# One step of a hybrid decoder layer on one core: cached keys handed over features leading, gathers spread over one-head-wide rows, gate groups moved between stages

## The chip, the cores and the metric

The kernel runs on one core of a Trainium2 chip. The time is device microseconds (us) of one execution, given as the median of several. A profile is one further execution, recorded by the hardware profiler; its span runs from its first to its last instruction. TensorE (PE) does matrix products, its weight loads (PEld) overlap them; VectorE (DVE), ScalarE (ACT) and GpSimd (POOL) do the element-wise work, SyncE (SP) issues most transfers. [...]

## The reference

288 tokens (a prompt of 256, and 8 sequences of 4 new tokens) go through one layer of width 4096. Cut to what matters:

```python
m = jax.nn.silu(c) @ w_ada + b_ada                  # (9, 4096) @ (4096, 12288): "adaLN"
shift, scale, gate = jnp.split(m[:, None, :], 3, axis=-1)
h = _rmsnorm(x, g_norm) * (1 + scale) + shift
(u_a, v_a, z_a, qkv_b, z_b, a_b, b_b, q_c, k_c, v_c, z_c, qi_c, ki_c, wi_c) = _split_in(h @ w_in)
...                                                  # mixer A: gMLP over chunks of 128, times silu(z_a)
qkv_conv, conv_new = _causal_conv(qkv_b, conv_prev, dn_conv_w)
o_b, s_new = _gated_delta(...)                       # mixer B: 16 heads, delta rule, times silu(z_b)
o_c = attend(q_c, k_c, v_c, qi_c, ki_c, wi_c)        # mixer C, times silu(z_c)
mix = jnp.concatenate([y_a, y_b, y_c], axis=-1)
x = x + gate * (mix @ w_out)                         # then a last RMSNorm

def _sparse_attend(q, k_sel, v_sel, valid):          # of mixer C, new tokens against their cache:
    s = jnp.einsum('bthgd,btkhd->bthgk', q, k_sel).astype(jnp.float32) * C_HEAD ** -0.5
    s = jnp.where(valid[:, :, None, None, :], s, -jnp.inf)
    p = jax.nn.softmax(s, axis=-1)
    return jnp.einsum('bthgk,btkhd->bthgd', p.astype(v_sel.dtype), v_sel)
```

The cache is paged: 8 sequences of 16 pages, a page being 128 positions of 2 key heads of 128 features (float32); a page table says which page of a pool of 160 is which. An indexer picks the keys that each query may see; the kernel scores all 2048 cached positions and masks the others.

## The kernel before

**Products.** All tokens stand as 288 columns. A weight tile of 128 x 1024 is loaded from HBM (`w`, four buffers, 512 KB a load), cast to a shorter float by ACT (`wh`), the rest is found by DVE (`wl`), and TensorE multiplies three times into one bank of PSUM (`acc`): hH by wh, hL by wh, hH by wl. A "block" is 128 output columns. Four of PSUM's banks (acc 0 to 3) are for these sums, four others for all else, which the code calls "banks". "A group" is four blocks (512 columns); the group called c, 112 columns of small things, is one block wide.

**Stages, in TensorE's order.** Stage 1 ("p1") computes m, with c as the stationary operand (`ada<-wa`, weight tiles `wa`, five buffers), interleaved with the first groups of the input projection. m arrives in order of the features, so the input projection is done here in 11 steps over the features (six of 2 tiles of 128, then five of 4); in each step every group of this stage adds its partial sum to SBUF (`part_finish`, DVE: `zb<-zb,acc`, `v_c` and the like). The groups are c, qi0, qi1, kv, qc0, qc1 and the gate groups that `PLAN["p1"]` names (zc: gates of mixer C, zb of B, za of A, each name 512 columns). Stage 2 takes the gate groups of `PLAN["attn"]`, then q, k and v of mixer B in four groups of heads (12 groups of columns, `qkv_finish`, `conv_gen`, each group's chain `dn_all`, DN[0] to DN[3]), then `PLAN["dn3"]`, then mixer A's v and u. The last stage multiplies the mix by w_out, eight groups, features in the order KB = 2, 3, 4, 5, 6, 7, 0, 1 (blocks of 512; each is loaded as `mx` from `mixD` and split into mH and mL by `mix_gen`). The gate third of m (`ada<-w`) is spread over stage 2.

**Who decides the order.** The products of the weights follow a written list of units. Everything else (attention, delta rule, indexing, gathers) runs as generators which a planner, `Weaver`, advances between these units by a clock of its own, with a guessed time for each instruction and transfer (`note_dma`: a gather counts as landed 4 us after its issue). `W.finish([...])` at a unit emits the rest of a chain there, with no weight product in between: `end_prev` does it for DN[g-2] at the end of group g's q columns, `gmlp_open` for DN[3], at unit 12 of mixer A's last u group. All engines execute in their own program order.

**The cached keys** (`sample_gen`, two halves of four sequences). Per half, 16 gathers on POOL's queue fetch 128 rows of 4 KB each (`kraw`; four positions of both heads in a row, row numbers `ixk` made by `idx_prompt`'s part for the cache). Each is transposed by 8 products with the identity (`kT`), copied from PSUM by DVE and ACT (`ktk`) and multiplied with the queries (`S<-ktk,qS`, 16 matmuls of 32 rows), then copied into S by ACT twice. The values come in 32 gathers per half of 128 rows of 2 KB (`vraw`), used as they are. POOL also does 1/9 of each convolution (`tap`, `cv`, 32 columns).

Of the kernel before, what the change touches and what calls it, by code (L numbers as in the profile page):

```python
# [12 lines left out]
I32 = mybir.dt.int32  # L13
AF = mybir.ActivationFunctionType
OP = mybir.AluOpType
# [24 lines left out]
N_RAW, N_ADA, N_SPLIT = 4, 5, 4  # L40
# [6 lines left out]
LEAD0 = 0  # L47
GMO = 12
# [5 lines left out]
PLAN = {"p1": ["zc0", "zc1", "zb0", "zb1", "zb2", "zb3"], "attn": ["za0", "za1"], "dn3": []}  # L54
# [36 lines left out]
class Weaver:  # L91
# [98 lines left out]
    def note_dma(self, key, out, ins):  # L190
        t = self.t
        t[key] = max([t[key], self.at(out, but="D"), self.at(out, None, self.reads), self.born.get(out.tensor.name, 0.0)] +
                     [self.at(x) for x in ins]) + (1.0 if key == "G" else 0.05)
        q = t[key]
        if key != "G":
            n = self.n_dma % 8
            q = t[key] = max(q, self.lanes[n])
            q = t["H"] = max(t["H"], q) + 0.45
        d = out.shape[0] * _size(out) * 4 / 360e3
        if key == "G":  # L200
            e, t["D"] = max(t["D"], q + 0.6) + d, t["D"] + d
        else:
            e = t["D"] = max(t["D"], q + 0.6) + d
            self.lanes[n] = e + 1.2
            self.n_dma += 1

        self.used(self.parts, out, e + (4.0 if key == "G" else 2.0), "D")
        for x in ins:
            self.used(self.reads, x, e + 1.2, "D")
# [172 lines left out]
def tile_hybrid_step(ctx: ExitStack, tc: tile.TileContext, I, O):  # L382
# [79 lines left out]
    class Gemm(Unit):  # L462
# [21 lines left out]
        def mm(self, j):  # L484
            us = [self.with_, self] if self.with_ else [self]
            if j == 0 and us[0].first:
                self.st.acc = {}
            off, m = self.tiles[j]
            if us[0].first:
                self.st.acc[j] = acc_tile(j)  # L490
            acc = self.st.acc[j]
            for u in us:
                kk = u.kk
                xh, xl = self.XH[kk // 4][:, kk % 4], self.XL[kk // 4][:, kk % 4]
                a, b = u.wh[:, off:off + m], u.wl[:, off:off + m]
                T.matmul(acc[:m, :NTOK], a, xh, start=u.first, stop=False)
                T.matmul(acc[:m, :NTOK], a, xl, start=False, stop=False)
                T.matmul(acc[:m, :NTOK], b, xh, start=False, stop=u.last)
            if self.last:
                self.finish(j, acc)  # L500
# [369 lines left out]
    while i < len(lb):  # L870
        rate, nxt = max([((min(len(la), la_end[j] + LEAD) - n) / (at_[j] - at_[i]), j) for j in range(i + 1, len(lb))],
# [269 lines left out]
    def idx_sample_gen():  # L1141
# [7 lines left out]
        sub16 = tl("ap", [P, 1], "sub16")  # L1149
        V.memset(sub16, 0.0)  # L1150
        sv = tl("ap", [P, 4], "sv")
        V.memset(sv, 16.0)

        for q in range(4):
            G.affine_select(sv[:, q:q + 1], sv[:, q:q + 1], pattern=[[0, 1]], compare_op=OP.is_ge, fill=0.0,
                            base=-32 * q - 16, channel_multiplier=1)
            G.affine_select(sv[:, q:q + 1], sv[:, q:q + 1], pattern=[[0, 1]], compare_op=OP.is_ge, fill=0.0,
                            base=32 * q + 31, channel_multiplier=-1)
# [9 lines left out]
        ptm = pts[:, 384:448].rearrange("p (b j) -> p b j", j=16)  # L1168
        G.memset(ptm, 0.0)
        for u in range(2):  # L1170
            G.affine_select(ptm, ptm, pattern=[[-32, 4], [-1, 16]], compare_op=OP.not_equal, fill=1.0,
                            base=-16 * u, channel_multiplier=1)
# [5 lines left out]
        V.tensor_reduce(sub16, sv, axis=AX.X, op=OP.max)  # L1178
        ptf = tl("ap", [P, 3], "ptf")
# [4 lines left out]
        V.tensor_tensor(ptT.rearrange("p (h n) -> p h n", h=2), ptF.rearrange("p (h n) -> p h n", h=2),  # L1184
                        pts[:, 384:448][:, None].to_broadcast([P, 2, 64]), op=OP.mult)
        V.tensor_reduce(ptf[:, 1:3], ptT.rearrange("p (h n) -> p h n", h=2), axis=AX.X, op=OP.add)
# [5 lines left out]
        X.ixk = tl("ap", [P, 2, 16], "ixk", 1, I32)  # L1192
        for hf in range(2):
            V.tensor_scalar(ptf[:, 1 + hf:2 + hf], ptf[:, 1 + hf:2 + hf], 32.0, sub16, op0=OP.mult, op1=OP.add)
            V.tensor_scalar(X.ixk[:, hf], iof, ptf[:, 1 + hf:2 + hf], None, op0=OP.add)
# [208 lines left out]
    def sample_gen():  # L1404
        yield lambda: hasattr(X, "qready")
        k_rows = I["cache_k"][0].rearrange("n (e l) h d -> (n e) (l h d)", e=32)
# [3 lines left out]
        def gather_k(hf, s):  # L1410
            raw = tl("ap", [P, 4, 256], "kraw", 2)
            G.indirect_dma_start(out=raw.rearrange("p l c -> p (l c)"), out_offset=None, in_=k_rows,
                                 in_offset=bass.IndirectOffsetOnAxis(ap=X.ixk[:, hf, s:s + 1], axis=0))
            return raw
# [16 lines left out]
        for hf in range(2):  # L1431
# [3 lines left out]
            raws = [gather_k(hf, 0), gather_k(hf, 1)]  # L1435

            def qk_lane(par):
                raw = raws[par]
                for s in range(par, 16, 2):
                    yield [raw]  # L1440
                    yield from bank(2)
                    pk = [pr4("kT") for _ in range(2)]
                    for kv in range(2):
                        for l in range(4):
                            T.transpose(pk[kv][:, l], raw[:, l, kv * HD:(kv + 1) * HD], ident)
                    if s + 2 < 16:
                        raw = gather_k(hf, s + 2)
                    yield [pk[1]]
                    kt = tl("ap", [P, 2, 4, P], "ktk", 2, tag="kt")
                    V.tensor_copy(kt[:, 0], pk[0])  # L1450
                    A.copy(kt[:, 1], pk[1])
                    free(2)
                    yield from bank()
                    ps = pr("S")
                    qk_mm(ps, P, hf, lambda kv, bb: kt[:, kv, :, 32 * bb:32 * bb + 32])
                    yield
                    dst = Sk[:, 4 * (s % 4):4 * (s % 4) + 4].rearrange("p l (j u w) -> p l w u j", u=2, w=4)[:, :, s // 4]
                    for u in range(2):
                        A.activation(dst[:, :, u], ps[:, 0:P].rearrange("p (l u j) -> p u l j", l=4, u=2)[:, u], AF.Copy,
                                     scale=HD ** -0.5)  # L1460
                    free()

            ls = W.push(qk_lane(0), qk_lane(1), front=True)
            yield lambda: all(x.done for x in ls)
# [915 lines left out]
_INS = ["x_prompt", "x_sample", "cache_k", "cache_v", "cache_kidx", "state_dn_t", "state_conv_t", "page_table",  # L2380
# [9 lines left out]
def lay_out(inputs):  # L2390
# [3 lines left out]
    a = dict(inputs)  # L2394
    a["state_conv_t"] = np.asarray(a.pop("state_conv"))[0].reshape(24, 12, 4, P).transpose(1, 3, 2, 0)
# [52 lines left out]
```

## Time and profile before

| what | value |
|---|---|
| time, median of 3 runs | 2605.29 us (2603.06 to 2607.48) |
| the profiled execution's own time | 2601.98 us |
| its span | 2600.3 us |
| TensorE busy | 2498.2 us (96%) |
| VectorE, ScalarE, GpSimd busy | 1622.6, 1055.8, 478.0 us |
| granted TensorE clock, mean | 0.983 |
| moved over DMA | 615.88 MB, mean 237 GB/s |

A busy time is the sum of an engine's instructions in the span; matrix products overlap each other, so the mean of one (296 ns) is longer than the step from one to the next.

### The profile page before, as it was taken

How to read it: one execution, taken by the hardware profiler on the slowest of the kernel's cores; microseconds unless marked ns; L12 is line 12 of the kernel's file. 1: busy time of each engine (PE TensorE's matmuls, PEld its weight loads, DVE VectorE, ACT ScalarE, POOL GpSimd, SP SyncE). 2: the span in 40 equal slices, each digit the busy share in tenths (PEclk: the TensorE clock that was granted, in tenths of full speed). 3: DMA queues.
4: the chain of work that ended last, by engine and by line, in shares of the span. 5: the costliest groups of instructions: out<-in, count | busy, mean ns of one | idle time of the engine just before them, and what ended most of it. 6: DMA issues, size and time to landing. Idle time of an engine off the chain costs nothing. (4 is left out here: it accounts for less than half of the span.)

```text
span 2600.3 us, 51897 instructions
## 1 busy us (share of the span) xinstructions
PE 2498.2 (96%) x19572; PEld 2232.4 (86%) x19572; DVE 1622.6 (62%) x3616; ACT 1055.8 (41%) x2446; POOL 478.0 (18%) x1096
## 2 busy tenths in 40 slices
PE   5999999999999999999999999999999998999997
PEld 3788888888897788888899889989989988999997
DVE  3377765555568798555576576667567566555554
ACT  3423223323344434344444444444454534444443
POOL 1000000000001122534533333443330200000000
PEclk9999999999999999999999999999999999999998
DMA  7988988887656567877776565666666455555554
GB/s 281 369 328 340 343 321 316 314 326 298 220 182 207 169 224 255 284 255 259 252 261 204 171 224 204 203 218 222 200 219 236 143 198 163 188 173 177 177 186 162
DMA packets 207947, 615.88 MB, mean 237 GB/s; under 512 B 41901, under 2 KB 61841, under 8 KB 207697
## 3 DMA queue, kind: packets, MB, share of 16 engines
q1 hardware_dynamic: 196816, 574.82, 62.7%
q0 software_dynamic: 10880, 37.76, 4.2%
q8 instruction: 154, 2.52, 0.4%
q14 instruction: 97, 0.79, 0.1%
HBM read 587.54 MB, written 24.95 MB: 236 GB/s over the span
## 5 line engine op out<-in xcount | busy, mean ns | idle before, releaser
L74 DVE TENSOR_TENSOR wl<-w,wh 128x512 fp32r<-128x512 f32 (+1 forms) x1216 | 801.3, 682 | 672.9 <-ACT wh L74 662.9
L74 ACT CAST wh<-w 128x512 fp32r<-128x512 f32 (+1 forms) x1216 | 712.0, 611 | 1131.7 <-PE acc L74 816.0
L74 PE MATMUL acc<-hH,wh 128*128 128x288 f32 (+1 forms) x3744 | 1151.7, 308 | 20.2 <-ACT hH L74 8.7
L74 PE MATMUL acc<-hH,wl 128*128 128x288 f32 (+1 forms) x3744 | 1109.2, 296 | 1.4 <-DVE wl L74 1.3
L74 PE MATMUL acc<-hL,wh 128*128 128x288 f32 (+1 forms) x3744 | 1109.2, 296 | 0.6 <-DVE hL L74 0.6
L74 PEld LDWEIGHTS acc<-hH,wh 128*128 128x128 f32 (+1 forms) x3744 | 707.0, 189 | 137.7 <-issue 72.1
L74 PEld LDWEIGHTS acc<-hH,wl 128*128 128x128 f32 (+1 forms) x3744 | 708.0, 189 | 5.1 <-DVE wl L74 5.1
L74 PEld LDWEIGHTS acc<-hL,wh 128*128 128x128 f32 (+1 forms) x3744 | 708.5, 189 | 1.3 <-DVE hL L74 1.2
L74 PE MATMUL acc<-mH,wh 128*128 128x288 f32 x1024 | 304.6, 297 | 7.5 <-ACT mH L74 7.5
L74 PE MATMUL acc<-mL,wh 128*128 128x288 f32 x1024 | 302.6, 296 | 0.8 <-DVE mL L74 0.8
L74 PE MATMUL acc<-mH,wl 128*128 128x288 f32 x1024 | 302.8, 296 | 0.0
L74 PEld LDWEIGHTS acc<-mH,wh 128*128 128x128 f32 x1024 | 192.9, 188 | 8.0 <-ACT mH L74 7.7
L74 PEld LDWEIGHTS acc<-mL,wh 128*128 128x128 f32 x1024 | 193.0, 188 | 1.1 <-DVE mL L74 1.1
L74 PEld LDWEIGHTS acc<-mH,wl 128*128 128x128 f32 x1024 | 193.0, 189 | 0.0
L74 PE MATMUL ada<-wa,cT 128*32 128x512 f32 x1024 | 135.3, 608 | 23.9 <-DVE bs L74 18.0
L74 DVE TENSOR_TENSOR zb<-zb,acc 128x288 f32<-128x288 f32 x160 | 70.3, 451 | 43.3 <-PE acc L74 43.0
L74 PEld LDWEIGHTS ada<-wa,cT 128*32 128x32 f32 x1024 | 28.4, 110 | 80.3 <-issue 44.1
L74 POOL TENSOR_TENSOR htmp<-yT,gaT 128x32 f32<-128x32 f32 x20 | 7.8, 388 | 449.0 <-ACT wh L74 335.3
L74 POOL TENSOR_SCALAR frs<-frs 128x1 f32<-128x1 f32 (+1 forms) x3 | 0.9, 297 | 456.0 <-DVE frs L74 455.9
L74 DVE TENSOR_TENSOR R<-R,R 128x248 f32<-128x248 f32 (+30 forms) x248 | 72.7, 293 | 10.4 <-DMA R<-dD 3.9
L74 POOL DMA_INDIRECT vraw<-in_cache_v_dram,ixv x64 | 66.4, 1038 | 42.1 <-issue 13.9
L74 DVE SCALAR_TENSOR_TENSOR cv<-xp,vecs,cv 128x256 f32<-128x256 f32 x144 | 70.9, 492 | 3.6
(443 smaller groups left out, 2342.3 us busy)
## 6 DMA issues: line engine op xcount, KB each, us to landing
w<-in_w_in_t_dram SPq DMA_DIRECT2D x464, 512.0 KB, 4.7
wa<-in_w_ada_t_dram SPq DMA_DIRECT2D x256, 512.0 KB, 6.1
w<-in_w_ada_t_dram SPq DMA_DIRECT2D x128, 512.0 KB, 5.7
w<-in_w_out_t_dram SPq DMA_DIRECT2D x128, 512.0 KB, 3.5
St<-in_state_dn_t_dram SPq DMA_DIRECT2D x16, 512.0 KB, 6.2
out_dram<-St SPq DMA_DIRECT2D x16, 512.0 KB, 3.7
X<-in_x_prompt_dram SPq DMA_DIRECT2D x8, 512.0 KB, 7.1
XF<-in_x_prompt_dram SPq DMA_DIRECT2D x16, 256.0 KB, 5.2
```

The source lines that it names most:

```text
L74: r = f(*a, **k)
```

## The change

The host hands the cache over as `cache_k_t` (page, feature, head, position). A row of it is one feature of one page: 256 numbers, 1 KB. 128 gathers of 128 such rows replace the 32 of 4 KB; what lands has the features on the partitions, so the 256 transposes and the copies of their results fall away, and two pages share one bank of PSUM and one copy. `ixk` becomes one number per feature and page. The planner counts a gather as landed 6 us after its issue. `kraw` lies in both tags, four buffers as before. `N_ADA` gives `wa` seven buffers; the last block of adaLN units is planned 8 units earlier (`LAST_LEAD`); group c sums into bank 2 instead of 0; and PLAN moves zb2, zb3 from stage 1 to stage 2's start, and za0, za1 to its place after q, k, v.

```diff
-N_RAW, N_ADA, N_SPLIT = 4, 5, 4
+N_RAW, N_ADA, N_SPLIT = 4, 7, 4
+LAST_LEAD = 8
-PLAN = {"p1": ["zc0", "zc1", "zb0", "zb1", "zb2", "zb3"], "attn": ["za0", "za1"], "dn3": []}
+PLAN = {"p1": ["zc0", "zc1", "zb0", "zb1"], "attn": ["zb2", "zb3"], "dn3": ["za0", "za1"]}
@@ note_dma
-        self.used(self.parts, out, e + (4.0 if key == "G" else 2.0), "D")
+        self.used(self.parts, out, e + (6.0 if key == "G" else 2.0), "D")
@@ group
-                self.st.acc[j] = acc_tile(j)
+                self.st.acc[j] = acc_tile(j if len(self.tiles) > 1 else 2)
@@ order of the units of stage 1
-        rate, nxt = max([((min(len(la), la_end[j] + LEAD) - n) / (at_[j] - at_[i]), j) for j in range(i + 1, len(lb))],
+        rate, nxt = max([((min(len(la), la_end[j] + LEAD) - n) /
+                         (at_[j] - at_[i] - (LAST_LEAD if la_end[j] == len(la) else 0)), j) for j in range(i + 1, len(lb))],
...
-        X.ixk = tl("ap", [P, 2, 16], "ixk", 1, I32)
-        for hf in range(2):
-            V.tensor_scalar(ptf[:, 1 + hf:2 + hf], ptf[:, 1 + hf:2 + hf], 32.0, sub16, op0=OP.mult, op1=OP.add)
-            V.tensor_scalar(X.ixk[:, hf], iof, ptf[:, 1 + hf:2 + hf], None, op0=OP.add)
+        X.ixk = tl("ap", [P, P], "ixk", 1, I32)
+        V.tensor_scalar(X.ixk, ptF, 128.0, iop[:, 0:1], op0=OP.mult, op1=OP.add)
@@ sample_gen
-        k_rows = I["cache_k"][0].rearrange("n (e l) h d -> (n e) (l h d)", e=32)
+        k_rows = I["cache_k_t"].rearrange("n d h k -> (n d) (h k)")
-        def gather_k(hf, s):
-            raw = tl("ap", [P, 4, 256], "kraw", 2)
-            G.indirect_dma_start(out=raw.rearrange("p l c -> p (l c)"), out_offset=None, in_=k_rows,
-                                 in_offset=bass.IndirectOffsetOnAxis(ap=X.ixk[:, hf, s:s + 1], axis=0))
+        def gather_k(hf, j):
+            raw = tl("ap", [P, 4, 2, P], "kraw", 2, tag="kt" if j % 2 else "kraw")
+            for bb in range(4):
+                i = 16 * (4 * hf + bb) + j
+                G.indirect_dma_start(out=raw[:, bb].rearrange("p h k -> p (h k)"), out_offset=None, in_=k_rows,
+                                     in_offset=bass.IndirectOffsetOnAxis(ap=X.ixk[:, i:i + 1], axis=0))
...
-            raws = [gather_k(hf, 0), gather_k(hf, 1)]
-                    for kv in range(2):
-                        for l in range(4):
-                            T.transpose(pk[kv][:, l], raw[:, l, kv * HD:(kv + 1) * HD], ident)
-                    kt = tl("ap", [P, 2, 4, P], "ktk", 2, tag="kt")
-                    V.tensor_copy(kt[:, 0], pk[0])
-                    A.copy(kt[:, 1], pk[1])
-                    qk_mm(ps, P, hf, lambda kv, bb: kt[:, kv, :, 32 * bb:32 * bb + 32])
...
+            raws = [gather_k(hf, j) for j in range(4)]
+            for s in range(8):
+                two = [raws.pop(0), raws.pop(0)]
+                yield two
+                yield from bank()
+                ps = pr("S")
+                for jj in range(2):
+                    qk_mm(ps[:, jj * P:jj * P + P], P, hf, lambda kv, bb: two[jj][:, bb, kv])
+                if s < 6:
+                    raws += [gather_k(hf, 2 * s + 4), gather_k(hf, 2 * s + 5)]
+                yield
+                A.activation(Sk[:, :, 16 * s:16 * s + 16].rearrange("p c k -> p k c"),
+                             ps[:, 0:2 * P].rearrange("p (k c) -> p k c", c=16), AF.Copy, scale=HD ** -0.5)
+                free()
@@ host
+    a["cache_k_t"] = np.asarray(a.pop("cache_k"))[0].transpose(0, 3, 2, 1)
```

How the planner then orders the instructions shows in three places. The first is POOL's queue in the second half of the sample attention; `kraw` is a gather of keys, `tap`, `cv` and `SSG` are a convolution's, `xp` its input. Before:

```order
L74 COPY SSG<-cv 128x32
L74 DMA kraw<-in_cache_k_dram,ixk 128x1024 x4
L74 MEMSET xp 128x3
L74 COPY xp<-scT 128x8x3
L74 DMA kraw<-in_cache_k_dram,ixk 128x1024
L74 MEMSET xp 128x3
L74 COPY xp<-scT 128x8x3
L74 DMA kraw<-in_cache_k_dram,ixk 128x1024
```

After the change, at the same place:

```order
L75 COPY SSG<-cv 128x32
L75 DMA kraw<-in_cache_k_t_dram,ixk 128x256 x16
L75 TENSOR_SCALAR cv<-xp,vecs 128x32
L75 TENSOR_SCALAR tap<-xp,vecs 128x32
L75 TENSOR_TENSOR cv<-cv,tap 128x32
L75 DMA kraw<-in_cache_k_t_dram,ixk 128x256 x8
L75 TENSOR_SCALAR tap<-xp,vecs 128x32
L75 TENSOR_TENSOR cv<-cv,tap 128x32
L75 TENSOR_SCALAR tap<-xp,vecs 128x32
L75 TENSOR_TENSOR cv<-cv,tap 128x32
L75 DMA kraw<-in_cache_k_t_dram,ixk 128x256 x8
```

One gather now brings one page of one sequence. Sixteen stand first, then eight for every two tiles that TensorE has used; 27 small operations of the convolutions stand between the first and the last of the half's 64 gathers.

The second place is TensorE's queue where DN[0], the first delta-rule chain of mixer B, ends with the new tokens' part (sT to Sup; `o`, `v` and `oT` are of the prompt's part). Before, weight products (acc) stand between its short bursts:

```order
L74 MATMUL acc_17337<-hH_5763,wl 128x288
L74 MATMUL sT<-ident,SSG 128x128 x3
L74 MATMUL acc_17306<-hH_5763,wh 128x288
L74 MATMUL acc_17306<-hL_5872,wh 128x288
L74 MATMUL acc_17306<-hH_5763,wl 128x288
L74 MATMUL acc_17320<-hH_5763,wh 128x288
```

After the change this part stands at the end of the q columns of the third group of heads, where `end_prev` finishes DN[0]:

```order
L75 MATMUL acc_15475<-hH_6878,wl 128x288
L75 MATMUL o_16343<-R_14845,R_14842 128x128
L75 MATMUL o_16343<-R_14845,K_14264 128x128
L75 MATMUL v_16350<-R_15646 128x128
L75 MATMUL v_16350<-R_14842 128x128
L75 MATMUL v_16350<-R_15646,cv 128x128
L75 MATMUL oT_16354<-ident,R_14841 128x128 x2
L75 MATMUL o_16360<-R_14845,K_14264 128x128
L75 MATMUL o_16360<-R_14845,R_14842 128x128
L75 MATMUL oT_16380<-ident,R_14845 128x128 x2
L75 MATMUL sT<-ident,SSG 128x128 x3
L75 MATMUL kbT<-ident,R_16385 128x128
```

The chain's 44 bursts, from `o` to the last `Sup`, follow each other there with no weight product in between; before, only its last 22 (oTs and Sup) did.

The third place is SP's queue as the last stage opens (`mx<-mixD_160` to `_165` are features 2 to 7 in units of KB; `vtk` is an output). Before:

```order
L74 DMA w<-in_w_out_t_dram 128x1024
L74 DMA mx<-mixD_160 128x1152
L74 DMA w<-in_w_out_t_dram 128x1024
L74 DMA mx<-mixD_161 128x1152
L74 DMA w<-in_w_out_t_dram 128x1024 x5
L74 DMA out_dram<-vtk 32x1024
L74 DMA mx<-mixD_163 128x1152
L74 DMA w<-in_w_out_t_dram 128x1024 x3
L74 DMA mx<-mixD_162 128x1152
```

After the change (blocks 2 and 3 stand a little earlier, among the last loads of w_in; `z` are gates of mixer A):

```order
L75 DMA w<-in_w_out_t_dram 128x1024
L75 DMA mx<-mixD_162 128x1152
L75 DMA w<-in_w_out_t_dram 128x1024 x7
L75 DMA out_dram<-vtk 32x1024
L75 DMA w<-in_w_out_t_dram 128x1024
L75 DMA mx<-mixD_163 128x1152
L75 DMA z_26303<-zD_151 128x288
L75 DMA w<-in_w_out_t_dram 128x1024 x2
L75 DMA z_26429<-zD_151 128x288
L75 DMA w<-in_w_out_t_dram 128x1024
L75 DMA mx<-mixD_164 128x1152
L75 DMA z_26454<-zD_151 128x288
```

The load of feature block 4 (`_162`) stands behind 1 load of w_out instead of 10, that of block 5 behind 9 instead of 7, that of block 6 behind 12 instead of 10.

## Rows read from the trace of the kernel before

**Rows 1.** Page of the profile: busy time of each engine with its share of the span, and its number of instructions.

```profile
PE 2498.2 (96%) x19572; PEld 2232.4 (86%) x19572; DVE 1622.6 (62%) x3616; ACT 1055.8 (41%) x2446; POOL 478.0 (18%) x1096
```

**Rows 2.** The chain that ended last (start, length, what), in the last stage, and a table of busy time by stretch (start:end, length, busy time of each engine and instructions, granted clock, DMA share, GB/s) for the same stage.

```profile
2228.05 44.15 PE acc L74 x333
...
2220.00:2500.00 280.00, 280.00 (x2126) 279.58 (x2125) 149.16 (x247) 116.82 (x208) 0.00 (x0) 1.00 0.55 177
```

**Rows 3.** Groups of TensorE's instructions over the whole span: tile out<-in, partitions x elements, count, busy time, mean ns of one, idle time before them and what ended it. Of `ada` two records stand for one instruction, of `S` too.

```profile
L74 PE MATMUL ada<-w,cT 128*32 128x512 f32 x512 | 68.2, 604 | 0.0
L74 PE MATMUL kT<-ident,kraw 128*128 128x128 f32 x256 | 33.5, 274 | 0.4 <-DMA kraw<-in_cache_k_dram,ixk 0.4
...
L74 PE MATMUL S<-ktk,qS 128*32 128x128 f32 x512 | 20.6, 279 | 0.0
```

**Rows 4.** What TensorE waited for, over the whole span: total us, times, longest.

```profile
PE acc L74 <- ACT hH L74: 8.7, 2, 4.5
PE acc L74 <- ACT mH L74: 7.5, 1, 7.5
PE acc L74 <- DVE v_c L74: 7.4, 7, 1.4
PE oTs L74 <- DVE R L74: 7.0, 2, 3.8
PE ada L74 <- DMA wa<-in_w_ada_t_dram: 5.9, 5, 2.3
```

**Rows 5.** Busy time by stretch, as in rows 2, at the four places where the granted clock falls in the stages that the change touches.

```profile
700.00:720.00 20.00, 13.97 (x79) 11.39 (x78) 9.47 (x24) 5.45 (x11) 2.21 (x8) 0.79 0.38 131
1490.00:1516.00 26.00, 22.96 (x84) 13.76 (x83) 15.77 (x57) 8.96 (x37) 10.91 (x36) 0.67 0.29 105
2095.00:2115.00 20.00, 16.82 (x76) 11.44 (x75) 12.64 (x46) 4.60 (x18) 1.58 (x4) 0.74 0.57 202
2160.00:2180.00 20.00, 11.71 (x60) 10.55 (x60) 12.58 (x28) 6.50 (x12) 0.00 (x0) 0.74 0.50 170
```

**Rows 6.** TensorE in time (start, length, instruction, idle before it and what ended it) around 705 us, the start of stage 1's last step.

```profile
706.76 0.66 PE L74 MATMUL ada<-ident,adasb 128*128 128x128 f32 x4 [0.70 <-ACT adasb L74]
711.90 0.58 PE L74 MATMUL acc<-hH,wh 128*112 128x288 f32 x1 [4.48 <-ACT hH L74]
...
713.07 0.44 PE L74 MATMUL acc<-hH,wl 128*112 128x288 f32 x1
713.31 0.44 PE L74 MATMUL acc<-hH,wh 128*112 128x288 f32 x1
```

**Rows 7.** The chain that ended last, around 2165 us, at the start of the last stage (rows between them left out).

```profile
2153.57 7.24 PE acc L74 x53
...
2160.88 0.63 ACT wh L74
...
2162.63 4.56 DMA mx<-mixD
...
2169.81 1.57 PE acc L74 x5
```

**Rows 8.** Stage 1, 100 to 300 us: busy time by stretch; TensorE's groups in it; and GB/s in 40 slices of it.

```profile
100.00:300.00 200.00, 198.15 (x1477) 161.28 (x1477) 139.61 (x310) 64.30 (x122) 8.47 (x32) 1.00 0.89 342
...
L74 PE MATMUL acc<-hH,wh 128*128 128x288 f32 x375 | 113.4, 302 | 1.7 <-ACT wh L74 1.0 <-DVE v_c L74 0.6
...
L74 PE MATMUL ada<-wa,cT 128*32 128x512 f32 x336 | 43.2, 599 | 0.2 <-DMA wa<-in_w_ada_t_dram 0.2
...
GB/s 402 329 380 356 404 407 197 351 371 407 151 398 337 388 300 384 318 401 265 359 288 417 295 386 325 397 297 384 357 264 242 410 412 302 300 393 337 342 318 308
```

**Rows 9.** Groups of GpSimd's instructions over the whole span, and from the views of the two gathered tiles the durations (ns, min/median/max) (for keys, then for values), and for keys the time from issue to landing.

```profile
L74 POOL TENSOR_SCALAR tap<-xp,vecs 128x32 f32<-128x32 f32 x144 | 72.5, 503 | 0.4
L74 POOL DMA_INDIRECT vraw<-in_cache_v_dram,ixv x64 | 66.4, 1038 | 42.1 <-issue 13.9 <-PE kT L74 12.2 <-PE so L74 10.9
L74 POOL TENSOR_TENSOR cv<-cv,tap 128x32 f32<-128x32 f32 x144 | 49.9, 346 | 12.0
...
L74 POOL DMA_INDIRECT kraw<-in_cache_k_dram,ixk x32: 934/952/1427, 897.3 to 1181.0; - x32
...
DMA to landing us min/median/max: 4.6/5.6/7.7
...
L74 POOL DMA_INDIRECT vraw<-in_cache_v_dram,ixv x64: 942/948/1491, 1029.5 to 1259.3; - x64
```

**Rows 10.** GpSimd in time: gathers of values one behind another, around 1065 us.

```profile
1063.75 1.19 POOL L74 DMA_INDIRECT vraw<-in_cache_v_dram,ixv  x1 [0.30 <-issue]
1065.25 1.08 POOL L74 DMA_INDIRECT vraw<-in_cache_v_dram,ixv  x1 [0.30 <-issue]
```

**Rows 11.** VectorE's groups between 1059 and 1190 us, the second half of the sample attention.

```profile
L74 DVE TENSOR_TENSOR wl<-w,wh 128x512 fp32r<-128x512 f32 x52 | 35.3, 692 | 47.2 <-ACT wh L74 45.5 <-PE S L74 1.5
...
L74 DVE TENSOR_SCALAR cv<-xp,vecs 128x256 f32<-128x256 f32 x7 | 2.5, 355 | 0.0
```

**Rows 12.** TensorE in time from 1465 us: one chain of new tokens' delta rule (its own rows; the weight products between them left out).

```profile
1465.33 0.49 PE L74 MATMUL sT<-ident,SSG 128*128 128x128 f32 x3
...
1474.37 1.08 PE L74 MATMUL kS<-St,R 128*32 128x128 f32 x32
...
1489.24 0.33 PE L74 MATMUL oTs<-ident,R 128*128 128x128 f32 x1 [3.84 <-DVE R L74]
```

More of the change, by code (lines that the diff above doesn't have):

```diff
@@ L1148, in idx_sample_gen @@
         G.iota(iof, pattern=[[1, 16]], base=0, channel_multiplier=0, allow_small_or_imprecise_dtypes=True)
[L1149 to L1158, printed above, removed]
         iop = tl("ap", [P, 2], "iop")
@@ L1166, in idx_sample_gen @@
         V.tensor_scalar(iop[:, 1:2], iop[:, 1:2], 8.0, None, op0=OP.mult)
[L1168 to L1172, printed above, removed]
         ptj = pts[:, 448:464]
@@ L1177, in idx_sample_gen @@
         yield [ptB]
-        V.tensor_reduce(sub16, sv, axis=AX.X, op=OP.max)
-        ptf = tl("ap", [P, 3], "ptf")
+        ptf = tl("ap", [P, 1], "ptf")
         ptvf = tl("ap", [P, NB], "ptvf")
@@ L1183, in idx_sample_gen @@
         V.tensor_reduce(ptf[:, 0:1], ptT, axis=AX.X, op=OP.add)
-        V.tensor_tensor(ptT.rearrange("p (h n) -> p h n", h=2), ptF.rearrange("p (h n) -> p h n", h=2),
-                        pts[:, 384:448][:, None].to_broadcast([P, 2, 64]), op=OP.mult)
-        V.tensor_reduce(ptf[:, 1:3], ptT.rearrange("p (h n) -> p h n", h=2), axis=AX.X, op=OP.add)
         V.tensor_tensor(ptT.rearrange("p (b j) -> p b j", j=16), ptF.rearrange("p (b j) -> p b j", j=16),
@@ L1434, in sample_gen @@
             Sk = S[:, 0:2048].rearrange("p (c k) -> p c k", k=P)
-            raws = [gather_k(hf, 0), gather_k(hf, 1)]
[L1437 to L1442, printed above, removed]
-                    for kv in range(2):
-                        for l in range(4):
-                            T.transpose(pk[kv][:, l], raw[:, l, kv * HD:(kv + 1) * HD], ident)
-                    if s + 2 < 16:
-                        raw = gather_k(hf, s + 2)
-                    yield [pk[1]]
-                    kt = tl("ap", [P, 2, 4, P], "ktk", 2, tag="kt")
-                    V.tensor_copy(kt[:, 0], pk[0])
-                    A.copy(kt[:, 1], pk[1])
-                    free(2)
-                    yield from bank()
-                    ps = pr("S")
-                    qk_mm(ps, P, hf, lambda kv, bb: kt[:, kv, :, 32 * bb:32 * bb + 32])
[L1456 to L1464, printed above, removed]
+            raws = [gather_k(hf, j) for j in range(4)]
[12 more added lines that the diff above has]
+                free()
             raws = []
@@ L2377, in tile_hybrid_step @@
     close_pool("fp")
-_INS = ["x_prompt", "x_sample", "cache_k", "cache_v", "cache_kidx", "state_dn_t", "state_conv_t", "page_table",
+_INS = ["x_prompt", "x_sample", "cache_k_t", "cache_v", "cache_kidx", "state_dn_t", "state_conv_t", "page_table",
         "c_t", "vecs_t", "w_ada_t", "w_in_t", "w_in_c", "a_vnorm", "a_ws_t", "a_bs",
```

## The prediction

> **What bounds the kernel now.** I read the page's busy times first: TensorE is busy for 96% of the span and no other engine for more than 62% [rows 1]. The chain that ended last shows what that means: in the last stage it runs through weight products alone, 333 in 44.15 us, so one takes 0.1326 us, and in 280 us TensorE is never idle [rows 2]. So a TensorE instruction removed is worth its whole step, and everything else is worth nothing until TensorE waits for it. Next come the groups of TensorE's instructions [rows 3], for the price of what goes, and its waits [rows 4], which are few. [...]
>
> The profiled execution took 2601.98 us, of which 2600.3 are its span. The sum below is made against it; the median is 3.3 us higher, and I add that at the end. Changes of less than 0.2% (5.2 us) can't be told from none here.
>
> **Gains.** (a) The 256 transposes kT go, 33.5 us [rows 3]. They stand among weight products in stretches that TensorE fills, so I count 33 (28 if some cover waits). The products S stay 256 (two records each), so their 20.6 us stays. The 32 copies ktk, 48 of the copies of S and 80 additions of partial sums (zb2, zb3 no longer add up in steps) leave DVE and ACT, which nobody waits for there: 0.
>
> (b) After the single block of group c, the next group needs the bank that DVE is still reading: 7.4 us in 7 waits for v_c [rows 4]. With c in bank 2, two blocks, 12 products or 1.6 us, lie between. New is that c itself waits for bank 2 of the group ahead of it, with one block (0.8 us) between. I take -5, between 0 and -7.4.
>
> (c) At the start of stage 1's last step TensorE waits 0.70 and 4.48 us until h of the last features exists [rows 6]; the stretch has 6.0 us idle and a clock of 0.79 [rows 5]. In the new order the last adaLN products stand 96 weight products (12.7 us) ahead of that step, so the wait and its low clock go: -10 (6.0 to 10.6).
>
> (d) `gmlp_open` no longer finds anything of DN[3] to finish: its oTs and Sup stand among weight products. That stretch has 3.2 us idle and a clock of 0.74 [rows 5]: -6 (3.2 to 7.8).
>
> (e) The last stage begins with 7.5 us of waiting for mH of feature block 4 [rows 4]. The chain shows why: its load stands in SP's queue behind 10 loads of w_out, and a load there waits until the weights four loads ahead of it have been split, so it is issued only as TensorE ends the products of the fourth load; from there to the next product are 9.0 us (cast, split, 4.56 us of transfer, two conversions) [rows 7]. Now this load stands behind one, so the 8.3 idle us and some 2.8 of low clock go [rows 5]. But block 6 now stands behind 12, and its products begin with the ninth load: it leaves as the sixth is used up, two loads (24 products, 3.2 us each) ahead of need, and 9.0 - 6.4 = 2.6 us late. Block 5, behind 9 and needed with the seventh, has 9.6 us and is just in time. Net -8.5 (4 to 11).
>
> Together -62.5.
>
> **Losses.** (f) POOL must issue 128 gathers instead of 32. No row shows one of 128 rows of 1 KB; those of 4 KB take 0.952 us and those of 2 KB 0.948, both of 128 rows [rows 9], so the size of a row did not matter, and I take the same. Back to back they follow at 1.25 to 1.5 us, with 0.30 us between them [rows 10]; the mean is 1.04 + 0.30 = 1.34. The second half needs 64 x 1.25 to 64 x 1.34 = 80 to 86 us, plus 27 operations of the convolutions at about 0.36 (9.7 us; tap 0.503, cv 0.346, the others less) [rows 9] queued among them, plus 5.6 us for the last to land: 95 to 101 us. From the last use of the first half's values, when its buffers come free, to the last S, TensorE has 504 weight products (66.8 us), 20 adaLN products of 0.264 (5.3), 128 S of 0.08 (10.3) [rows 3] and 2 us of small ones: 84 us. So it waits 11 to 17 us. In the first half, some 590 products and 17 us of others make 95 us against the same 95 to 101: 0 to 6. I take 17 for both and 5 for the clock: +22, between 0 (TensorE's side is larger than I think, or the gathers start earlier) and 45.
>
> (g) The whole chain of DN[0] for the new tokens, and the end of the prompt's, is now finished in one piece, with nothing between its bursts. From sT to oTs one such chain takes 23.9 us in the trace [rows 12]. Its own TensorE work is 17 small products of 0.13 and four bursts of 1.08, 6.5 us; 17 are idle, and about 3 more for the prompt's last steps. 3.8 of it were already there. I take +16; 8 if the steps between run faster with the engines less loaded, 25 with the clock and the load of the gates inside the chain. DVE's and ACT's casts of weights queue behind it only until their four buffers are full.
>
> (h) The short steps of stage 1 lose 16 of 90 tile blocks, that is 48 of 270 products (6.4 us) and 1.05 MB, but keep the adaLN loads. In 200 us there are 1125 products, 4.17 steps [rows 8]: one is 48.0 us and 16.4 MB, and becomes 41.6 us and 15.4 MB, or 370 GB/s where 342 flow now. 342 isn't the ceiling: TensorE is busy 198 of these 200 us, and slices of 5 us reach 417 [rows 8]. At 342 each of the six steps would wait 3.4 us, 20 in all; with nothing 0. Seven buffers cushion it: +5.
>
> Losses +43; net -19.5: 2601.98 - 19.5 = 2582.5 for the profiled execution, **2586 us** as a median.
>
> [...] A gather of values took at most 1.49 us against 0.94 at least [rows 9], and in the second half VectorE spends 35.3 us in two-input subtractions and 2.5 us in operations of a tensor with scalars [rows 11]. [...]
>
> **Rivals.** *Gathers and loads hidden.* POOL starts early enough in both halves and stage 1's loads keep up; of the losses only DN[0] remains. For it speaks that TensorE's side (84 us) is only 11 us short, against it that both halves must come out well. 2586 - 17 - 5 - 5 = 2559.
>
> *Gathers held up.* If a gather of keys issues at the pace of the slow ones, TensorE waits (64p + 15.3 - 84) + (64p + 15.6 - 95) us for a pitch p: 23 at p = 1.34, 44 at 1.5, 81 at 1.79 (1.49 + 0.30, all as slow as the slowest). With 5 to 8 for the clock in place of my 22, that is 2613 at 1.5 and 2653 at 1.79; it is slower than before by more than 0.2% from a pitch of 1.48. For it speaks that single gathers of 1.2 to 1.5 us are common [rows 10]; against it that the median is 0.95.
>
> *Stage 1 becomes bound by its loads.* At 342 GB/s throughout: 20 instead of 5, 2601; no change that can be told. For it the mean share of 0.89, against it the slices above 400 [rows 8].
>
> **How the numbers follow.** My forecast, with its own range of 2572 to 2602, has 0.43; all hidden 0.25; gathers held up 0.18 (mostly above 2610); loads bound 0.14. Faster: 0.85 of the first and all of the second make 0.62; the rest of the first and most of the loads' case are the same, 0.17; gathers held up past 1.48 and the far ends of the others are slower, 0.21. The range leaves out the far ends of the two outer cases: 2556 to 2618.
>
> **What would show it.** No kT in the profile after; TensorE waiting in S for kraw, a few us each time, 17 in all, and POOL's gathers one behind another with 0.3 us between them at a pitch near 1.3; a run of short idle pieces before oTs in the third group of heads, 16 us in all, and a low clock there; no wait for hH at the last step nor for R at `gmlp_open`; mH waited for by some 2.6 us instead of 7.5; v_c gone from the waits; in stage 1 few waits for wa and about 365 GB/s. I am wrong if a gather of 1 KB rows costs much more or much less than one of 4 KB, if the chain of DN[0] is far longer than 24 us, or if the moved gate groups open a wait that I have not looked for.

## The result and the profile after

The changed kernel takes 2630.88 us (median of 4 runs, 2624.78 to 2633.26) where the kernel before took 2605.59 beside it: 1.009 times, 95% interval 1.0072 to 1.0108. It is slower by about 25 us, or 1%; the forecast was 2586, faster. Its profiled execution took 2632.66 us, 30.7 more than the one before.

The page's span, busy times and granted clock (in tenths of the full clock, 40 slices of the span), to be read beside [rows 1]:

```profile
span 2630.9 us, 51203 instructions
...
PE 2497.7 (95%) x19316; PEld 2222.9 (84%) x19316; DVE 1572.3 (60%) x3496; ACT 1037.5 (39%) x2358; POOL 566.7 (22%) x1181
...
PEclk9999999999998999999996999999999999999998
```

TensorE is busy as long as before (2497.7 us against 2498.2) although 33.5 us of transposes are gone [rows 3]: what it does runs at a lower clock, and its idle time grew, from 102.0 to 133.2 us. The clock records of both profiles know two levels, the full clock (1.00) and half of it (0.50): 147.3 us of the span are at half clock, 91.7 before. What it waited for (total us, times, longest), beside [rows 4]:

```profile
PE acc L75 <- issue: 18.3, 28, 1.5
PE kbT L75 <- ACT R L75: 9.2, 7, 4.5
PE S L75 <- issue: 8.4, 15, 1.0
...
PE acc L75 <- ACT hH L75: 4.2, 1, 4.2
...
PE oT L75 <- DVE R L75: 3.0, 1, 3.0
...
PE oTs L75 <- DVE R L75: 2.8, 1, 2.8
...
PE acc L75 <- DVE mL L75: 2.1, 1, 2.1
...
PE ada L75 <- DMA wa<-in_w_ada_t_dram: 1.6, 7, 0.2
...
PE S L75 <- DMA kraw<-in_cache_k_t_dram,ixk: 1.0, 1, 1.0
...
PE acc L75 <- ACT mH L75: 0.4, 1, 0.4
```

The waits for v_c are gone, hH, mH and wa have shrunk. New is "issue": pauses in which TensorE waited for nothing that the records show. Before, no pause above 0.1 us was without a releaser; now there are 28.8 us of them, counting each gap for which no semaphore event is on record (the rows above leave out gaps under 0.15 us and add gaps whose event came over 1 us earlier). 22.4 us of the 28.8 stand before products that wait on no semaphore at all; the other 6.4 may be waits whose record is missing. 26.7 us lie in the two stretches of key gathers, whose clock is 0.88 and 0.89; the third place with a low clock is DN[0]'s chain (by stretch: start:end, length, busy us of PE, PEld, DVE, ACT, POOL, clock, DMA share, GB/s; beside [rows 5, 8]):

```profile
100.00:300.00 200.00, 198.19 (x1487) 158.88 (x1486) 142.62 (x323) 60.55 (x111) 11.73 (x40) 1.00 0.96 368
807.00:900.00 93.00, 77.46 (x594) 63.43 (x593) 62.34 (x119) 26.55 (x68) 46.27 (x48) 0.88 0.63 201
1035.00:1128.00 93.00, 74.30 (x611) 62.34 (x611) 25.49 (x43) 25.24 (x53) 64.45 (x88) 0.89 0.66 214
1385.00:1450.00 65.00, 48.60 (x308) 32.69 (x307) 27.86 (x101) 22.96 (x100) 23.96 (x71) 0.68 0.21 67
```

The stages, from the products that open each in the two traces, with the products moved between them taken out at 0.1326 us each, against what the forecast's terms give for each:

| stage | change forecast | change measured |
|---|---|---|
| stage 1 (b, c, h) | -10 | -24.8 |
| its end to the last use of values in the sample attention (a, f) | -11 | +38.2 |
| from there to the last stage (d, g) | +10 | +21.5 |
| last stage (e) | -8.5 | -4.2 |
| sum | -19.5 | +30.7 |

So the miss of 50 us is the sample attention's 49. The other misses (-15, +12 and +4) cancel, which is luck.

How a pause looks (TensorE and POOL in time, second half of the key gathers; rows of other products and PEld left out):

```profile
1038.86 0.95 POOL L75 DMA_INDIRECT kraw<-in_cache_k_t_dram,ixk  x1 [0.30 <-issue]
1039.50 0.29 PE L75 MATMUL acc<-hH,wl 128*128 128x288 f32 x1 [1.11 <-issue]
...
1039.63 0.29 PE L75 MATMUL acc<-hH,wh 128*128 128x288 f32 x1
...
1040.11 0.95 POOL L75 DMA_INDIRECT kraw<-in_cache_k_t_dram,ixk  x1 [0.31 <-issue]
...
1041.63 0.44 PE L75 MATMUL acc<-hH,wl 128*128 128x288 f32 x1 [1.13 <-issue]
...
1042.61 0.95 POOL L75 DMA_INDIRECT kraw<-in_cache_k_t_dram,ixk  x1 [0.31 <-issue]
```

A product that waits on no semaphore starts 1.1 us after the one ahead of it has ended, then two come together, then another gap, on a grid of about 0.7 us; POOL's gathers meanwhile follow each other every 1.25 us. A product that stands alone also takes 0.29 us of the engine where in a row it takes 0.13, so the pauses cost more than their length. VectorE and ScalarE have no gap over 0.2 us there before an instruction that waits on no semaphore.

### The profile page after: what moved, and what is told of

It reads as the page before. It is cut to its first block, busy times and chain, and to the rows that moved or that the text cites. A ratio compares the mean times of both kernels' runs of the same rounds, so it can differ in the third digit from the quotient of the medians.

```text
span 2630.9 us, 51203 instructions
## 1 busy us (share of the span) xinstructions
PE 2497.7 (95%) x19316; PEld 2222.9 (84%) x19316; DVE 1572.3 (60%) x3496; ACT 1037.5 (39%) x2358; POOL 566.7 (22%) x1181
## 5 line engine op out<-in xcount | busy, mean ns | idle before, releaser
L75 POOL DMA_INDIRECT kraw<-in_cache_k_t_dram,ixk x128 | 126.1, 985 | 93.1 <-PE S L75 42.3
L75 PE MATMUL ada<-w,cT 128*32 128x512 f32 x512 | 74.5, 619 | 3.0 <-issue 2.9
```

Source lines behind the costliest of these rows:

```text
L75: r = f(*a, **k)
```

## The experiments

The runs were made on four chips, called A (e1 to e4), B (e5, e6), C (e7 to e10) and D (e11 to e14); e15 had a fifth. On which chip the first result was taken is not on record. The kernel before ran beside each: medians 2603.40, 2605.13, 2603.76, 2609.01 and 2603.23. All times below are medians; "pauses" are the gaps of TensorE without a releaser, counted as above.

### Which part of the change

**e1, all but the keys:** the kernel before with the new numbers, PLAN, bank and lead; gathers, transposes and the planner's 4 us as before.

```diff
-N_RAW, N_ADA, N_SPLIT = 4, 5, 4
+N_RAW, N_ADA, N_SPLIT = 4, 7, 4
+LAST_LEAD = 8
+PLAN = {"p1": ["zc0", "zc1", "zb0", "zb1"], "attn": ["zb2", "zb3"], "dn3": ["za0", "za1"]}
...
```

> The kernel before with every edit except those to the keys (seven wa buffers, the earlier last adaLN block, bank 2 for group c, the moved gate groups): the keys come as 32 gathers of 4 KB rows with transposes, and the planner counts a gather as landed after 4 us. Theory 1 (the loss comes with the gathers of 1 KB rows): TensorE's pauses without a releaser are absent, stage 1 ends as early as after the change, and the time is 35 to 45 us below before, 2560 to 2570. Theory 2 (the loss comes with the moved gate groups): the long idle piece before oTs in the third group of heads is there too, and the time is at or above before, 2605 to 2620.

2578.58, ratio 0.990 (0.9873 to 0.9928), no pauses. Theory 1 is right in the sign; the gain is 25, not 35 to 45.

**e2, the keys alone:** the changed kernel with those lines undone.

> The kernel after the change with every edit undone except those to the keys and the planner's 6 us: gate groups, adaLN buffers and lead, and bank of group c as before. Theory 1: pauses of TensorE without a releaser in both stretches of key gathers, 25 to 30 us in all, and DN[0]'s chain in one piece: slower than before by 50 to 75 us, 2655 to 2680. Theory 2: the transposes' 33 us are gained, with 10 to 20 given back to waits for gathers: 2580 to 2595.

2607.24, ratio 1.0012 (0.9997 to 1.0028): on chip A no pauses, so neither theory's time. The two parts apart give -25 and +4, together they gave +25 elsewhere: something was different on this chip, which e3 and e4 showed too.

**e3, other rows,** and **e4, other prices in the planner:**

```diff
-        V.tensor_scalar(X.ixk, ptF, 128.0, iop[:, 0:1], op0=OP.mult, op1=OP.add)
+        V.scalar_tensor_tensor(X.ixk, iop[:, 0:1].to_broadcast([P, P]), 157.0, ptF, op0=OP.mult, op1=OP.add)
```

> The kernel after the change with other rows fetched: row 157 p + page for partition p instead of 128 page + p, so that the 128 rows of one gather lie 157 KB apart and not in one piece of 128 KB (the keys fetched are then not those of the page table's pages, which is the part of the computation that is changed). Theory 1a (rows of one page lie together in memory and the transfers stand in each other's way): the pauses of TensorE without a releaser go and with them 35 to 50 us, 2580 to 2596. Theory 1b (the number or rate of gathers does it, wherever the rows lie): the pauses stay at 25 to 30 us, 2620 to 2640.

```diff
-... (1.0 if key == "G" else 0.05)
+... (0.6 if key == "G" else 0.05)
-        self.used(self.parts, out, e + (6.0 if key == "G" else 2.0), "D")
+        self.used(self.parts, out, e + (4.0 if key == "G" else 2.0), "D")
```

> The kernel after the change with the planner's price of a gather lowered from 1.0 to 0.6 us on POOL and from 6 to 4 us to landing; the work is the same, but the sample attention ends 400 products earlier in the written order and DN[0]'s chain for the new tokens stands among weight products again (oTs 126 products ahead of the point where it would be forced). Theory A (the forced chain costs its idle time and the low clock behind it, 20 to 30 us): 2600 to 2612, and the idle piece of 16 us before oTs and the low clock there are gone. Theory B (POOL's gathers set the pace, so TensorE then waits for them at S): the wait for kraw rises from 1 us to 20 to 30 us, and the time stays at 2622 to 2640.

2594.97 (ratio 0.9969, 0.9954 to 0.9983) and 2581.13 (0.9913, 0.9881 to 0.9944), both with 0.1 us of pauses; e4 lies below what either of its theories said. Read alone, e3 says that the rows' place makes the pauses, and e4 that its order avoids them. Both readings fell with the runs on chips B and C.

### The chip

**e5, e7, e14: the changed kernel again; e8, e9, e10: e3, e4 and e2 again, beside it.**

> The changed kernel itself once more, on the chip and in the session of its companions. In its first profile TensorE pauses for 28.8 us in the stretches of key gathers without any releaser in the records, and no transfer's landing was recorded; kernels with the same gathers (keys only; other rows; other planner prices) show none of these pauses. Theory P (the pauses belong to this program, its order of gathers and products): they are there again, 20 us or more, and the time is again 2624 to 2634. Theory Q (they belong to that session or to where that copy of the program lay in memory): no pauses without a releaser, landings recorded, waits for kraw at S in their place, and 2590 to 2612; what is left against the planner's other prices (2581) is then the forced chain of DN[0].

> The changed kernel a third time, now on one chip with three kernels that showed no pauses so far but ran on another chip than its second run. Theory P (the pauses belong to the program: this order of gathers and products, with the rows of a page in one piece): pauses without a releaser of 25 to 35 us and 2624 to 2634 here as on the others. Theory U (they belong to the chip or the session, for any kernel with gathers of 1 KB rows): as its companions here, that is, all four with such pauses or all four without; without them 2595 to 2605.

> The kernel whose gathers fetch rows 157 KB apart (not the pages of the table, which is the part of the computation that is changed), beside the changed kernel on one chip. Theory P with the rows' place as its cause: no pauses, 2589 to 2602, some 35 us below the changed kernel. Theory U: the changed kernel's time within 8 us and as many pauses.

> The changed kernel with the planner's lower prices of a gather (0.6 and 4 us), beside it on one chip. Theory P: no pauses and 2577 to 2586. Theory U with pauses: 2605 to 2620, 25 us or more above its first run; without: 2577 to 2586, and the changed kernel at 2595 to 2605, so that DN[0]'s chain in one piece costs some 18 us.

> The edits to the keys alone (all else as before the change), beside the others on one chip. Theory P: no pauses, 2600 to 2613. Theory U with pauses: 2630 to 2650, since the pauses' 30 us and their low clock come on top of its first run; without: 2600 to 2613.

| kernel | chip A: us, pauses | chips B, C, D: us, pauses |
|---|---|---|
| changed kernel | not run | 2632.16, 32.6 (B); 2626.66, 26.7 (C); 2628.64, 28.8 (D) |
| other rows (e3, e8) | 2594.97, 0.1 | 2658.22, 36.2 (C) |
| other prices (e4, e9) | 2581.13, 0.1 | 2627.44, 43.9 (C) |
| keys alone (e2, e10) | 2607.24, 0.0 | 2656.81, 30.8 (C) |
| all but the keys (e1, e13) | 2578.58, 0.1 | 2581.99, 4.1 (D) |

Theory U: each kernel with 128 key gathers takes 46 to 63 us more on chip C than the same kernel on chip A. The kernel before does not (2603.76 against 2603.40), nor does e1 on chip D (2581.99 against 2578.58). Neither the rows' place nor the order is the cause. The sizes were missed: all three lie above what theory U said for a chip with pauses, e8 by 24 us, e9 and e10 by 7. On the chips that pause, the profile also lacks the landings of transfers (for the changed kernel the gather's duration, and its line among the transfers' issues, where the landing's us would stand at the end). Each transfer that lands leaves 16 events (the profile before has 22,301 for its 1,395 transfers); of the 23,856 for the changed kernel's 1,491, 2,901 are missing, nearly all between 700 and 1250 us, where the gathers are:

```profile
L75 POOL DMA_INDIRECT kraw<-in_cache_k_t_dram,ixk x128: 942/949/1427, 766.8 to 1123.6; - x128
...
kraw<-in_cache_k_t_dram,ixk POOLq DMA_INDIRECT x128
```

On chip A (e4, 23 events missing) the same line has 4.2 us, and TensorE waits for the gathers openly, 19.1 us, close to the 17 of the forecast:

```profile
PE S L75 <- DMA kraw<-in_cache_k_t_dram,ixk: 19.1, 17, 3.0
...
kraw<-in_cache_k_t_dram,ixk POOLq DMA_INDIRECT x128, 4.2
```

**e6, five wa buffers,** on chip B beside e5.

```diff
-N_RAW, N_ADA, N_SPLIT = 4, 7, 4
+N_RAW, N_ADA, N_SPLIT = 4, 5, 4
```

> The changed kernel with five wa buffers instead of seven; every product stands where it stood. Theory R (the two buffers are what lets stage 1 run without waiting for adaLN weights): waits for wa come back, 6 us or more, and the time is 5 to 15 us above the changed kernel in the same session. Theory S (TensorE sets the pace in stage 1 with either): waits for wa stay under 3 us and the time is the same within 5 us.

2649.74, 17.6 above the changed kernel there: theory R, and more than it said. The waits for wa themselves are 7.9 us; by the traces, stage 1 takes 22.9 us longer than in e5:

```profile
PE ada L75 <- DMA wa<-in_w_ada_t_dram: 7.9, 17, 1.3
```

### What in the gathers

**e11, the gathers spaced; e12, half as many of 2 KB; e13 and e14 beside them on chip D.**

```diff
...
                 G.indirect_dma_start(...)
+                G.obj.tensor_tensor(slow, slow, nhalf[:, 0:2], op=OP.pow)
```

> The changed kernel with an idle power of two numbers on POOL behind each gather of keys (0.74 us by the rows of such operations before), so that gathers follow at 2.0 us instead of 1.25; the planner does not see it, so every other instruction stands where it stood. Theory V (the pauses come when gathers follow each other without a break): on a chip where the changed kernel pauses, the pauses without a releaser fall under 8 us, while TensorE's waits for gathers grow: 64 x 0.75 us more per half, 60 to 95 us in all, 2660 to 2720. Theory W (each gather of 1 KB rows costs its pause whenever it comes): the pauses stay at 25 us or more.

```diff
...
+                if bb % 2 == 0:
+                    G.obj.indirect_dma_start(out=raw[:, bb:bb + 2].rearrange("p b h k -> p (b h k)"), out_offset=None, in_=k_rows2,
+                                             in_offset=bass.IndirectOffsetOnAxis(ap=X.ixk[:, i:i + 1], axis=0))
...
```

> The changed kernel with half as many gathers of keys, 64 of 128 rows of 2 KB (as the values' gathers are), the same bytes into the same tiles at the same places in the order (the rows are not those of the page table's pages, which is the part of the computation that is changed). Theory V and the number of gathers: no pauses, no waits for gathers worth 5 us, and 2575 to 2592. If the bytes or the new place of the gathers beside the other loads do it: pauses of 20 us or more remain and it is above 2600.

> All edits except those to the keys, once more, on a chip beside the changed kernel. No gathers of 1 KB rows, so no pauses on any chip: 2575 to 2583 as in its first run. If the pauses came from anything else in the change, it would be 2600 or more where the changed kernel is at 2625.

> The changed kernel on the chip of the three others, to tell whether this chip pauses at all: 2622 to 2635 with 25 to 33 us of pauses without a releaser, as on three chips before, or 2590 to 2605 without pauses, as its companions had on a fourth chip.

The changed kernel's waits on this chip, then e11's with POOL in time, then e12's:

```profile
PE acc L75 <- issue: 14.2, 20, 2.4
PE S L75 <- issue: 12.4, 17, 1.4
...
PE S L75 <- DMA kraw<-in_cache_k_t_dram,ixk: 3.5, 4, 1.1
```

```profile
PE S L75 <- DMA kraw<-in_cache_k_t_dram,ixk: 58.2, 39, 3.7
...
PE acc L75 <- issue: 0.4, 1, 0.4
...
1049.67 1.28 POOL L75 DMA_INDIRECT kraw<-in_cache_k_t_dram,ixk  x1 [0.18 <-issue]
1050.98 0.73 POOL L1401 TENSOR_TENSOR slow<-slow,nhalf 128x2 f32<-128x2 f32 x1
1051.89 1.02 POOL L75 DMA_INDIRECT kraw<-in_cache_k_t_dram,ixk  x1 [0.18 <-issue]
```

```profile
PE S L75 <- issue: 3.0, 6, 1.0
...
PE S L75 <- DMA kraw<-in_cache_k_t_dram,ixk: 1.4, 2, 1.2
...
PE acc L75 <- issue: 0.2, 1, 0.2
```

With 1.97 us (median) from gather to gather instead of 1.25, and the same gathers at the same places, the pauses fall from 28.8 to 0.9 us; the waits for kraw take over, 58.2 us, and the time is 2684.18. With half as many gathers, of 0.949 us each (median), and the same bytes in all, the pauses are 3.4 us, the waits go as well, and the time is 2568.83, 60 below the changed kernel on the same chip and a little below what was expected. Theory V fits both: on these chips the pauses come with many gathers close behind each other. How many, and whether the size of a row counts, is not separated: e12 has fewer gathers and longer rows. e13 is 2581.99 (ratio 0.9905, 0.9879 to 0.9931); its gathers of values, in runs of six to eight at 1.25 to 1.33 us, leave 4.1 us of pauses.

All of these runs lose records on chip D, and not equally: the changed kernel 3,012 of the landing events, e12 1,582, e11 1,396, e13 923. On chip A, without pauses, at most 75 are missing. So the kernel with by far the most pauses, 28.8 us, also lost the most records, the other three, with 3.4, 0.9 and 4.1 us, a third to a half as many; e11 and e12 thin the records with the gathers.

### The forced chain

**e15:** e1 with the planner's landing of a gather at 3 us.

```diff
-        self.used(self.parts, out, e + (4.0 if key == "G" else 2.0), "D")
+        self.used(self.parts, out, e + (3.0 if key == "G" else 2.0), "D")
```

> The kernel with all edits except those to the keys, and with the planner's price of a gather's landing at 3 us instead of 4, which lets the sample attention end some 140 products earlier in the written order; DN[0]'s oTs then stands 126 products ahead of the point where the chain would be forced, instead of in 25 forced bursts. [...] If the chain's waits only move elsewhere: 2575 to 2583.

2562.66 (2559.99 to 2567.44), ratio 0.9844 (0.9827 to 0.986): 16 below e1, a little more than the 8 to 14 us that I had worked out from e1's trace (3.8 us idle at the forced piece, and 24 us at half clock behind it that lose 8 to 11), and the fastest kernel of the study that leaves the computation as it is. The stretch of DN[0]'s end in e1 and a later one, and the clock of e15 in 40 slices:

```profile
1360.00:1395.00 35.00, 28.39 (x108) 17.96 (x108) 20.02 (x72) 14.23 (x62) 15.21 (x46) 0.66 0.25 91
1590.00:1616.00 26.00, 24.47 (x125) 19.36 (x127) 14.20 (x45) 11.58 (x45) 9.75 (x32) 0.74 0.54 176
```

```profile
PEclk9999999999999999999999999999999999999998
```

In e1 the clock over these 35 us is 0.66; in e15 only the last slice is below 9. Not all of the 16 us need be the forced piece: at the same weight product, e15 is 9 us ahead just behind DN[0]'s end, and 19 only behind the second stretch, where e1 has 13.7 us at half clock and e15 has none. The split is rough, since the chains' own products stand at other places in the two orders.

## Why the prediction was wrong

**(f) is the step that failed.** Its inputs were right: a gather of 1 KB rows takes 0.949 us and 0.30 lie between two, as [rows 9, 10] had it, and on chip A, where there are no pauses, TensorE waits 8.0 (e2), 13.0 (e3) and 19.1 us (e4) for them, against 17. What failed is the pricing: it counted the gathers only by what waits for them, up to 45 us. In the changed kernel TensorE waits 1.0 us for them and pauses 28.8 us without a releaser, mostly before products that wait on no semaphore. The trace before could not show this: at most eight of its gathers follow each other so closely, and only 19 of its landing events are missing. With the transposes' 33 taken back, the sample attention lost 71 us in place of (f)'s 22; on chip D, half the gathers in the same order (e12) make this stage 56 us shorter than the changed kernel's. The clock was mis-sized too: I had put 5 us on it, and that stage has 58.0 us at half clock, 13.7 before. On chip A e3 loses some 38 without pauses, within (f)'s bounds: the waits are short but many, and 37.5 us are at half clock. Its time, 2594.97, lies inside the forecast's range, but only because stage 1 gained more than forecast.

**The rivals.** "Gathers held up" ended on the right side for the wrong reason. The slowest gather took 1.427 us, and only 13 of the 128 took more than 1.05; what all of them took beyond the median adds up to 4.8 us. All 13 overlap a two-input subtraction of VectorE; those beside no VectorE instruction took at most 1.041. So some gathers beside a subtraction were slower, but by far too little for this rival; what slowed them the trace does not tell.

**(g)** The place and the idle time were right: 16.4 us idle between 1385 and 1450 us, forecast 16. TensorE in time there (its chain's rows with the longest waits):

```profile
1393.78 0.69 PE L75 MATMUL oT<-ident,R 128*128 128x128 f32 x2 [2.96 <-DVE R L75]
...
1399.56 0.47 PE L75 MATMUL kbT<-ident,R 128*128 128x128 f32 x1 [4.45 <-ACT R L75]
...
1413.67 0.34 PE L75 MATMUL oTs<-ident,R 128*128 128x128 f32 x1 [2.76 <-DVE R L75]
...
1419.79 2.07 PE L75 MATMUL Sup<-R,R 32*128 32x512 f32 x2 [2.07 <-ACT R L75]
```

Left out of the value was the clock, which I had only in its upper bound of 25: 0.68 over these 65 us, 41 us of them at half clock. e15 is 16 us faster than e1 without such a piece, some 9 of them at the piece itself (6.6 us idle, the longest wait 3.8, clock 0.66). The chain comes so late because the sample attention ends some 320 products later in the written order, also with the old PLAN (e2); with the planner's lower prices (e4) it ends earlier than before, and the forced piece is gone.

**(h)** had the wrong sign, as far as the stage tells it apart from (b) and (c). Stage 1 flows at 368 GB/s, as worked out (370), but without waits: 1.6 us for wa instead of 5.9. The two more buffers do that (e6: 17.6 us without them). Together with (b) and (c), whose waits are gone as forecast (v_c 7.4 to 0, hH 8.7 to 4.2 with only the first left), stage 1 gained 24.8. e1 shows the same stage 1.

**(d)** no wait for R at `gmlp_open`, and the clock is 1.00 from 1885 to 2200 us: right. **(e)** had the new wait at the wrong block. TensorE waits 0.4 + 2.1 us, but at the first product of the fourth block in the order, the 145th of the last stage with 48 to a block: that is block 5, which I had just in time. Block 6, worked out as 2.6 us late, has no wait, so the match of the sizes is luck. Block 5's load leaves SP at 2190.53 us and its packets are done at 2195.4, but ACT converts it only at 2201.44, behind other casts in its program order, which I had not counted:

```profile
2190.53 0.43 SPq L75 DMA_DIRECT2D mx<-mixD  x1
...
2201.11 0.43 ACT L75 CAST mH<-uv 128x288 fp32r<-128x288 f32 x1
2201.44 1.15 ACT L75 CAST mH<-mx 128x1152 fp32r<-128x1152 f32 x1
...
2202.64 0.40 PE L75 MATMUL acc<-mH,wh 128*128 128x288 f32 x1 [0.42 <-ACT mH L75]
2205.16 0.40 PE L75 MATMUL acc<-mL,wh 128*128 128x288 f32 x1 [2.12 <-DVE mL L75]
```

The gain was 4.2 rather than 8.5, since 10.2 us at half clock stayed. The low clock in (c), (d) and (e), up to 4.6 us a wait, was my estimate; no run shows it apart from the wait. What the traces show is 10.2 us at half clock at each of the three waits before, and in the changed kernel only those of (e).

**What stays open.** Whether the pauses are TensorE's instructions arriving late, or the recording of the run. All executions timed here were recorded (each has its span and clock). For late instructions the traces have no sign: the loads of 16 KB of instructions are 152 in the changed kernel and in e4 on chip A, with medians of 0.98 and 0.97 us; how long each waited to start is not recorded. For the recording speaks that pauses of more than 1 us in all come only in profiles that lack many records: 0.9 to 4.1 us with 923 to 1,582 missing, and 27 to 44 us with some 2,700 to 3,000. Against it as the only cause speaks that e11, e12 and e13 lost a third to a half as many and had only 0.9 to 4.1 us of pauses; this does not exclude it. All runs have records, so how the kernel does without them is not known. A run of sixteen gathers is not needed: in the changed kernel's first half the key gathers stand in runs of eight at 1.25 to 1.31 us with short breaks, and 9.1 us of pauses lie there. Distances between 1.25 and 1.97 us were not tried.

## What to carry to other kernels

Price a transfer issued by GpSimd by the run of issues it stands in, not by the one: four times as many gathers of a quarter of the size cost the same 0.95 us each, and where many follow closely the cost may fall on an engine that waits for none of them. Where a planner's clock decides the order, look for the chain that is pushed to a forced finish behind the slowed one, and price it with its low clock (here 0.68 over 65 us), not with its idle time alone. Apply the parts of such a change apart and on more than one chip: here the regrouping alone was worth 25 us, with one planner's number 41. The new key layout took back more than the 25 on three chips, and on the fourth added nothing to it (e4's 2581 and e3's 2595 against e1's 2579).

## What the runs showed of the hardware that was not expected

On three of four chips tried, 128-row gathers issued every 1.25 us, mostly in runs of eight to sixteen, came with pauses of TensorE, mostly of 0.3 to 1.5 us, on a grid of 0.7 us, 27 to 44 us in all, 22 to 38 of them before products that wait on no semaphore; spaced to 1.97 us they came with 0.9. Some 2,700 to 3,000 landing records were missing in each of these profiles, so that the recording had a part in the pauses is not ruled out. On the fourth chip the same kernels had none, and were 46 to 63 us faster, while the kernel before differed by less than 6 us among all of them.
